# A soft mixture-of-experts kernel on Trainium2: the differences "kept P1 minus P5" on GpSimd instead of VectorE

## The chip, the cores and the metric

The kernel runs on one core of one Trainium2 chip. The metric is device time in microseconds (us) of one execution, as a median of runs. Engines are named as the profile names them: PE is TensorE's matmul, PEld its weight load, DVE is VectorE, ACT is ScalarE, POOL is GpSimd and SP is SyncE.

## The reference

Every token's output is the sum over all eight experts of the expert's matrix product, weighted by a softmax of the token's router logits:

```python
# x [16, 512, 512], router_logits [16, 512, 8], expert_weights [8, 512, 2048], all float32
probs = softmax(router_logits, axis=-1)
for e in range(8):
    output += probs[:, :, e:e+1] * np.matmul(x, expert_weights[e])
```

There are 8192 tokens (16 x 512), and the output is [16, 512, 2048] float32.

## The kernel before, in words

**The arithmetic.** Because the sum over experts can be put into the contraction, the output is one product of a matrix Z (the tokens times their probabilities, for all experts side by side) and a matrix W (the experts' weights on top of each other). The kernel computes it by a scheme of Strassen's kind, with seven products of blocks instead of eight, on two levels and in places on a third. The outer products are P1 to P7; `right[r]` is the weight operand of Pr, `lefts[r, q]` the token operand. q counts 16 groups of 512 tokens; each group has an even and an odd block of 256 tokens (`HQ`). Inside one outer product the same scheme is applied again: its seven inner steps are run in the order `STEPS = (1, 5, 6, 2, 7, 3, 4)`, and a step is eight matmuls of 128 x 128 by 128 x 512 in f16 into one PSUM bank (line 712).

**P1, P5 and P6.** Each outer product of one q has four result tiles of 128 x 512 f32, called tn = (0,0), (1,1), (0,1), (1,0). P1 is computed early and its results are written to DRAM (`kept`). Later come P5 and P6: P6's result is laid onto a base, which is kept P1 minus P5 for the same q, tile by tile. So for each q and each tn there is one subtraction of two 128 x 512 f32 tiles in SBUF, written in place over the tile with kept P1: 64 in all. `Base.fetch` (line 780) loads a tile of kept P1 with a DMA from SP's queue; `joined` (line 1171) makes the subtraction.

**Stages.** Work is a list of stages, and a stage is one or two outer products whose steps alternate. The stages of P5 and P6 (lines 1148 to 1152) are: P5 of q = 0 and 1; P6 of q = 0 alone; fourteen pairs of P6 of q and P5 of q + 1; P6 of q = 15 alone. In a pair the steps are numbered as slots 0 to 13, even slots for P6 and odd slots for P5; in a stage of one product slots are 0 to 6. `run` (line 1105) walks through the slots: hooks of that slot first, then the eight matmuls, then `slack` (which pops DVE tasks from the queue), then the step's `post`.

**Posts.** `post` takes a step's result out of PSUM. For a product without a base, such as P5, most are ACT copies to an SBUF tile (`post_alone`, line 723); for P6 (`post_on_base`, line 743) all but step 2 are DVE additions of a PSUM bank and the base. In one of the pair stages the DVE posts are those of slots 0, 2, 4, 8, 9, 10, 11 and 12. Step 1 of P6 needs base (0,0), step 5 needs (1,1), step 6 needs (0,1), step 4 needs (1,0). Steps 1, 6, 7 and 4 of one product share one PSUM bank: the matmuls of step 6 add onto what step 1 left there, those of step 7 onto step 6, and so on, with the post of each in between. So the post of slot 4 (step 6 of P6) has to have read the bank before the matmuls of slot 8 (step 7 of P6) write to it; in a stage of one product, the post of slot 2 before slot 4.

**What sets the order.** Every engine runs its instructions in program order. DVE's order is planned by hand: left operands, sums of weights and the like are tasks with a cost in us (`later`, line 388), held in a queue; `slack` (line 401) keeps a clock for PE and one for DVE and pops tasks as far as DVE's clock allows. `joined` puts its subtraction at the head of that queue (`True`) with a cost of 0.69; `need` (line 383) runs it at the latest when P6's post asks for the base. Hooks call `joined` in the stage before the P6 concerned at slot 12 for (0,0), at slot 13 for (1,1) and (0,1), and in P6's own stage at slot 3 for (1,0); where the stage before has one product, at slots 5, 6, 6 and again 3 (lines 1180 to 1182). The fetches of kept P1 are at slots 2, 4, 6 and 7 of the stage before (1, 2, 3, 4 in a stage of one product).

**POOL's queue** holds DMAs alone in these stages: the stores of result tiles to the output (`to_out`, line 771, one after each finished tile), the loads of x that still has to be cast (`XBlock.begin`, line 420), loads of weights for later sums (`load_part`, `cast_part`) and stores of weight sums. `pool` (line 126) and `note` (line 101) issue them in program order.

**Buffers.** Base tiles and result tiles come from one pool of 12 tiles (`hpool`, tag `h`); SP's fetch of a base waits until a tile of this pool is free, that is until a store has landed or a last reader is done. Matmul results have 6 + 2 PSUM banks (`bank`, tile name `ps`; `bank2`, `pt`).

Of the kernel before, what the change touches and what calls it, by code (L numbers as in the profile page):

```python
# [31 lines left out]
def kernel(  # L32
# [7 lines left out]
    nc = tc.nc  # L40
# [3 lines left out]
    ADD, SUB, MUL = mybir.AluOpType.add, mybir.AluOpType.subtract, mybir.AluOpType.mult  # L44
# [38 lines left out]
    def half():  # L83
        return h_tile([P, NB], f32)
# [16 lines left out]
    def note(i):  # L101
        last[i.ins.engine] = i.ins
        if ordered[0]:
            tc.keep_in_program_order(i)

    def dve(i):
        last[i.ins.engine] = i.ins
        tc.keep_in_program_order(i)
# [3 lines left out]
    def tt(o, a, b, op):  # L112
        dve(nc.vector.tensor_tensor(out=o, in0=a, in1=b, op=op))  # L113
# [12 lines left out]
    def pool(o, i, **how):  # L126
        note(nc.gpsimd.dma_start(out=o, in_=i, **how))  # L127
# [203 lines left out]
    for n in range(2):  # L331
# [23 lines left out]
        for j in range(4):  # L355
            o = half()
# [22 lines left out]
    def flush(task):  # L379
        while task is not None and not task.done:  # L380
            queue.popleft().run()

    def need(task):
        if task is not None and not task.done:
            flush(task)
            clock["pe"] = max(clock["pe"], clock["dve"])

    def later(cost, make, first=False):
        t = Task(cost, make)
        (queue.appendleft if first else queue.append)(t)  # L390
        return t
# [375 lines left out]
    def out_rows(q, odd, cols, tn):  # L767
        t, n = tn
        return out_f[ds((2 * q + odd) * HQ + t * HP, HP), ds(cols * NH + n * NB, NB)]

    def to_out(q, odd, cols, **how):
        return lambda tn, o: pool(out_rows(q, odd, cols, tn), o, **how)
# [28 lines left out]
    right = {r: Right() for r in (2, 5, 6, 7, 4, 3)}  # L801
    right[1] = Right(w, {p: Task(2.29, sums[p]) for p in (6, 7, 4)})
    lefts, xs, ps_, bases = {}, {}, {}, {}
# [6 lines left out]
    def left_of(r, q, fresh=True):  # L810
        a, b = 2 * q, 2 * q + 1
        if r == 1:
            pt = PBlock(a, P1, xp1[q - 2][1] if q in (2, 3) else None)
            if q in (2, 3):
                xs[a] = XBlock(a, xp1[q - 2][0])
            return Left(xblock(a), pt), [xblock(a), pt]
        if r == 2:
            pt = PBlock(a, P2)
            return Left(xblock(a), pt), [xblock(a), pt]
        if r == 7:  # L820
            pt = PBlock(b, P2)
            if q >= KEPT_Z:
                return Left(xblock(b), pt, kept=lefts[6, q]), [xblock(b), pt]
            return Left(xblock(b), pt, onto=ZHalves(q)), [xblock(b), pt]
        if r == 4:
            return Left(lefts[7, q].xb, lefts[7, q].pb), []
        if r == 5:
            pt = PBlock(b, PQ)
            return Left(xblock(b), pt), [xblock(b), pt]
        if r == 6:  # L830
            pt = PBlock(a, P1)
            return Left(xblock(a), pt, of=lefts[5, q]), [xblock(a), pt]
        if r == 3 and (q, 0) in EARLY:
            sources = {k: operand3[q, k] for k in range(2) if (q, k) in EARLY}
            if len(sources) == 2:
                return LoadedLeft(None, None, None, sources), []
            pa = PBlock(a, P2)
            return LoadedLeft(xblock(a), pa, ZHalf(q, z_places[q]), sources), [xblock(a), pa]
        if r == 3 and q < KEPT_Z:
            pt, kept_z = PBlock(a, P2), ZBlock(q)  # L840
            return Left(xblock(a), pt, kept=kept_z), [xblock(a), pt, kept_z]
        pa, pb = PBlock(a, PQ), PBlock(b, PQ)
        return Left(xblock(a), pa, (xblock(b), pb)), [xblock(a), pa, xblock(b), pb]

    def kept_rows(q):
        return lambda tn: kept[q][tn[1], ds(tn[0] * HP, HP), :]

    def product(r, q, **how):
        left, loads = left_of(r, q)
        lefts[r, q] = left  # L850
        p = None
        if r == 1:
            def sink(tn, o):
                pool(kept_rows(q)(tn), o)
            p = Product(right[1], left, sink)
        elif r == 2:
            if q >= ON_BASE or q in WITH_KEPT:
                bases[2, q] = Base(kept_rows(q))
            p = Product(right[2], left, to_out(q, 0, 0), bases.get((2, q)))
        elif r == 5:  # L860
            bases[6, q] = m1 = Base(kept_rows(q))
            m1.task = {}

            p = Product(right[5], left, to_out(q, 1, 0))
        elif r == 6:
            m1 = bases[6, q]

            def base(tn):
                need(m1.task[tn])
                return m1.t[tn]  # L870
            p = Product(right[6], left, to_out(q, 0, 1), base)
        elif r == 7:
            base = products[6, q].o.__getitem__
            if q < KEPT_Z:
                base = bases[7, q] = Base(lambda tn: out_rows(q, 0, 1, tn))
            p = Product(right[7], left, to_out(q, 1, 1), base)
        elif r == 4:
            p = Product(right[4], left, to_out(q, 1, 0, accum_op=ADD), products[7, q].o.__getitem__)
        else:
            p = Product(right[3], left, to_out(q, 0, 1, accum_op=ADD), **how)  # L880
        p.loads = loads
        products[r, q] = p
        return p

    products = {}
# [251 lines left out]
    for q in range(2, 16, 2):  # L1137
        add(product(1, q), product(1, q + 1))
    xs.clear()
    for q in (2, 4, 0, 6, 8, 10, 12, 14):  # L1140
        add(product(2, q), product(2, q + 1))
    for q in (*WITH_KEPT, *range(ON_BASE, 16)):
# [3 lines left out]
        fetch_at(k, 3, bases[2, q], INNER[3])  # L1146
    xs.clear()
    k5 = add(product(5, 0), product(5, 1))
    add(product(6, 0))
    for q in range(1, 15):  # L1150
# [18 lines left out]
    at(k6 - 1, 7, lambda: claim(products[5, 15].o, (1, 0)))  # L1169

    def joined(q, tn):
        m1 = bases[6, q]
        m1.task[tn] = later(0.69, lambda: tt(m1.t[tn], m1.t[tn], products[5, q].o[tn], SUB), True)

    for q in range(16):
        k = k5 + 1 + q
        duo = len(stages[k - 1]) == 2
        for slot, tn in zip((2, 4, 6, 7) if duo else (1, 2, 3, 4), INNER):
            fetch_at(k - 1, slot, bases[6, q], tn)
        for tn, where in zip(INNER, ((k - 1, 12), (k - 1, 13), (k - 1, 13), (k, 3)) if duo  # L1180
                             else ((k - 1, 5), (k - 1, 6), (k - 1, 6), (k, 3))):
            at(*where, lambda q=q, tn=tn: joined(q, tn))
# [264 lines left out]
    for stage, slot, q, k in ((k3 - 1, 2, 11, 0), (k3 - 1, 5, 11, 1), (k3 - 1, 7, 8, 0), (k3 - 1, 9, 5, 0),  # L1447
                              (k3 - 1, 10, 8, 1), (k3 - 1, 12, 5, 1)):
        left = lefts[3, q]
# [191 lines left out]
```

## Time and profile before

| what | value |
|---|---|
| median of 3 runs | 1351.62 us (1351.12 to 1351.67) |
| the profiled execution's own time | 1351.78 us |
| its span, first to last instruction | 1350.1 us |
| PE, DVE, ACT, POOL busy in the span | 1344.0, 1166.9, 281.9, 403.9 us |
| granted TensorE clock | 1.0 |
| moved by DMA | 346.26 MB |

The profile is of one execution and its times are read against 1351.78 us, not against the median: 1.7 us of that lie before and after the span. A line of a group gives the kernel's line, the engine, the operation, the tiles written and read (buffer numbers left out), the shapes and the count; then the busy time in us and the mean duration of one in ns; then the engine's idle time just before these instructions and what ended it. L113 is the helper through which all DVE additions and subtractions go, L127 the helper of POOL's DMAs, L136 the helper of the matmuls, so groups are told apart by their tiles. A line of a timeline gives the start and the duration in us, then the instruction; instructions of one kind that follow each other are merged and counted.

### The profile page before, as it was taken

How to read it: one execution, taken by the hardware profiler on the slowest of the kernel's cores; microseconds unless marked ns; L12 is line 12 of the kernel's file. 1: busy time of each engine (PE TensorE's matmuls, PEld its weight loads, DVE VectorE, ACT ScalarE, POOL GpSimd, SP SyncE). 2: the span in 40 equal slices, each digit the busy share in tenths (PEclk: the TensorE clock that was granted, in tenths of full speed). 3: DMA queues.
4: the chain of work that ended last, by engine and by line, in shares of the span. 5: the costliest groups of instructions: out<-in, count | busy, mean ns of one | idle time of the engine just before them, and what ended most of it. 6: DMA issues, size and time to landing. Idle time of an engine off the chain costs nothing.

```text
span 1350.1 us, 19508 instructions
## 1 busy us (share of the span) xinstructions
PE 1344.0 (100%) x7122; PEld 694.3 (51%) x7122; DVE 1166.9 (86%) x1483; ACT 281.9 (21%) x593; POOL 403.9 (30%) x619
## 2 busy tenths in 40 slices
PE   9999999999999999999999999999999999999998
PEld 4465655565544444444444444554555455556564
DVE  7878898989989889797897889889898989898984
ACT  3342423223211111111111100110111111224331
POOL 3123322333323232323312112424334231232342
PEclk9999999999999999999999999999999999999999
DMA  9999989989899999999998889999999989999997
GB/s 181 242 222 240 239 264 242 291 284 290 247 329 282 323 288 286 295 306 265 318 325 265 295 313 189 243 239 216 244 249 226 219 219 310 308 178 230 262 163 132
DMA packets 185392, 346.26 MB, mean 256 GB/s; under 512 B 52176, under 2 KB 81616, under 8 KB 181200
## 3 DMA queue, kind: packets, MB, share of 16 engines
q0 software_dynamic: 84960, 176.72, 58.0%
q1 hardware_dynamic: 97024, 146.15, 35.4%
q10 hardware_dynamic: 3312, 22.15, 4.6%
q8 instruction: 55, 0.90, 0.3%
q14 instruction: 41, 0.34, 0.1%
HBM read 203.19 MB, written 174.26 MB: 280 GB/s over the span
## 4 chain that ended last, share of the span: by engine, by line
PE 98%; DMA 1%; POOL 0%; issue 0%; ACT 0%; POOLq 0%
PE ps L136 77%; PE pt L136 21%; DMA w<-in_expert_weights_dram 1%; POOL w L127 0%; ACT h L1578 0%; POOL ident L234 0%; POOLq L234 0%; POOLq L1625 0%
## 5 line engine op out<-in xcount | busy, mean ns | idle before, releaser
L136 PE MATMUL ps<-w,z 128*128 128x512 f16 (+1 forms) x3884 | 840.0, 372 | 0.0
L136 PEld LDWEIGHTS <-z 128*128 128x128 f16 x5236 | 512.3, 98 | 538.1 <-issue 1.1
L127 POOL DMA_DIRECT2D out_dram<-h x380 | 251.8, 679 | 723.9 <-ACT h L751 321.9
L113 DVE TENSOR_TENSOR h<-ps,h 128x512 f32<-128x512 f32 x318 | 214.9, 686 | 59.1 <-PE ps L136 58.0
L136 PE MATMUL pt<-w,z 128*128 128x512 f16 (+1 forms) x1304 | 253.2, 338 | 0.7 <-DMA w<-in_expert_weights_dram 0.7
L113 DVE TENSOR_TENSOR z<-xT,pT 128x2048 f16<-128x2048 f16 x188 | 226.8, 1217 | 2.2 <-DMA xT<-xs 2.2
L136 PE MATMUL ps<-w,d 128*128 128x512 f16 x880 | 200.7, 379 | 0.0
L738 ACT COPY h<-ps 128x512 f32<-128x512 f32 x102 | 59.8, 586 | 394.0 <-PE ps L136 394.0
L136 PEld LDWEIGHTS <-d 128*128 128x128 f16 x880 | 86.1, 98 | 96.3
L113 DVE TENSOR_TENSOR z<-z,d 128x2048 f16<-128x2048 f16 x110 | 131.8, 1217 | 0.0
L113 DVE TENSOR_TENSOR w<-w 128x1024 f16<-128x1024 f16 (+2 forms) x106 | 116.1, 1114 | 2.6 <-PE ps L136 1.0
L113 DVE TENSOR_TENSOR d<-z 128x1024 f16<-128x1024 f16 x110 | 74.1, 685 | 1.0
L113 DVE TENSOR_TENSOR h<-pt,h 128x512 f32<-128x512 f32 x75 | 51.3, 687 | 27.0 <-PE pt L136 23.9
L751 ACT COPY h<-ps 128x512 f32<-128x512 f32 x54 | 31.6, 586 | 203.5 <-PE ps L136 203.5
L113 DVE TENSOR_TENSOR ps<-ps,h 128x256 f32<-128x256 f32 (+1 forms) x84 | 50.6, 603 | 21.0 <-PE ps L136 15.1
L734 ACT COPY h<-ps 128x512 f32<-128x512 f32 x89 | 49.9, 599 | 70.1 <-PE ps L136 61.3
L127 POOL DMA_DIRECT2D kept<-h x56 | 30.6, 547 | 86.2 <-DVE h L113 48.7
L113 DVE TENSOR_TENSOR z<-z 128x2048 f16<-128x2048 f16 (+1 forms) x52 | 50.5, 978 | 1.5
L730 ACT COPY ps<-ps 128x512 f32<-128x512 f32 x47 | 26.8, 570 | 107.4 <-PE ps L136 59.5
L113 DVE TENSOR_TENSOR h<-h 128x512 f32<-128x512 f32 (+2 forms) x69 | 45.0, 675 | 0.1
L127 POOL DMA_DIRECT2D out_dram<-kept x40 | 42.0, 1150 | 0.2 <-issue 0.2
L136 PEld LDWEIGHTS <-h 128*128 128x128 f16 x384 | 37.6, 98 | 4.3
(109 smaller groups left out, 691.7 us busy)
## 6 DMA issues: line engine op xcount, KB each, us to landing
out_dram<-h POOLq DMA_DIRECT2D x380, 256.0 KB, 7.5
z<-z SPq DMA_DIRECT2D x56, 512.0 KB, 8.7
pT<-p_dram SPq DMA_DIRECT2D x93, 256.0 KB, 8.1
h<-kept SPq DMA_DIRECT2D x88, 256.0 KB, 7.2
w<-wd ACTq DMA_DIRECT2D x20, 1024.0 KB, 8.6
w<-in_expert_weights_dram POOLq DMA_DIRECT2D x33, 512.0 KB, 12.2
xT<-x SPq DMA_DIRECT2D x63, 256.0 KB, 7.8
h<-out_dram SPq DMA_DIRECT2D x60, 256.0 KB, 8.9
```

The costliest lines, as they stand in the source:

```text
L113: dve(nc.vector.tensor_tensor(out=o, in0=a, in1=b, op=op))
L127: note(nc.gpsimd.dma_start(out=o, in_=i, **how))
L136: note(nc.tensor.matmul(ps, z, w, start=start, stop=stop, skip_group_check=True))
L730: act(nc.scalar.copy(self.banks["b"], x))
L734: act(nc.scalar.copy(o[tn], q if p == 5 else x))
L738: act(nc.scalar.copy(o[TN[p]], b if p == 2 else x))
L751: act(nc.scalar.copy(o[tn], b))
```

## The change

The 64 subtractions are issued on GpSimd, directly at their hooks, and no longer pass through the queue of DVE tasks. With that, the tasks kept per tile of the base (`m1.task`) and the function that asked for them before a post go away; a post of P6 gets the tile and waits, on the engine, for the instruction that wrote it.

```diff
         elif r == 5:
-            bases[6, q] = m1 = Base(kept_rows(q))
-            m1.task = {}
-
+            bases[6, q] = Base(kept_rows(q))
             p = Product(right[5], left, to_out(q, 1, 0))
         elif r == 6:
-            m1 = bases[6, q]
-
-            def base(tn):
-                need(m1.task[tn])
-                return m1.t[tn]
-            p = Product(right[6], left, to_out(q, 0, 1), base)
+            p = Product(right[6], left, to_out(q, 0, 1), bases[6, q])
...
     def joined(q, tn):
-        m1 = bases[6, q]
-        m1.task[tn] = later(0.69, lambda: tt(m1.t[tn], m1.t[tn], products[5, q].o[tn], SUB), True)
+        o = bases[6, q].t[tn]
+        note(nc.gpsimd.tensor_tensor(out=o, in0=o, in1=products[5, q].o[tn], op=SUB))
```

The hooks and their slots, the fetches of kept P1 and everything else stay as they are. In POOL's program order a subtraction now stands where its hook stands: that of (0,0) behind the store that follows the post of slot 11, those of (1,1) and (0,1) between the stores that follow the posts of slots 12 and 13, that of (1,0) behind the loads that the early slots of P6's stage issue.

## The prediction

> **What bounds the kernel now.** First the page: engine shares, the chain that ended last, and the row of base loads, needed below.
>
> ```profile
> span 1350.1 us, 19508 instructions
> ## 1 busy us (share of the span) xinstructions
> PE 1344.0 (100%) x7122; PEld 694.3 (51%) x7122; DVE 1166.9 (86%) x1483; ACT 281.9 (21%) x593; POOL 403.9 (30%) x619
> ...
> PE 98%; DMA 1%; POOL 0%; issue 0%; ACT 0%; POOLq 0%
> ...
> h<-kept SPq DMA_DIRECT2D x88, 256.0 KB, 7.2
> ```
>
> PE is busy all the time and is the chain. A busy matmul row can still hide a slow pipeline, so I next read the stretch in which the change acts: the fourteen pair stages of P6 and P5, from 428.7 to 767.1 us, in the view of windows, and then the same stretch grouped by form.
>
> ```profile
> 428.70:767.10 338.40, 338.40 (x1569) 153.43 (x1568) 287.86 (x350) 48.42 (x83) 95.45 (x168) 1.00 0.99 296
> ```
> ```profile
> L136 PE MATMUL ps<-w,z 128*128 128x512 f16 x897 | 198.3, 379 | 0.0
> ...
> L136 PE MATMUL pt<-w,z 128*128 128x512 f16 x448 | 101.3, 379 | 0.0
> ...
> L136 PE MATMUL ps<-w,d 128*128 128x512 f16 x224 | 50.6, 379 | 0.0
> ```
>
> The columns of the window are its length, then PE, PEld, DVE, ACT and POOL busy, the granted clock, DMA share and GB/s. The three groups are all of the window's 1569 matmuls, with 0.0 us idle before each: 338.40 / 1569 = 215.7 ns from one to the next. So a slot of eight takes 1.725 us, a pair stage of 14 slots 24.2 us, and no wait of PE is left in the stretch. DVE is busy for 287.86 of 338.40 us, 85%, yet nothing waits for it long enough to stop PE. **Taking work from DVE can therefore give PE nothing back here**; the question is whether the new place makes PE wait.
>
> **Where a pair stage has slack.** I take the stage that begins at 622 us; DVE first, from its timeline.
>
> ```profile
> 619.28 0.68 DVE L113 TENSOR_TENSOR h<-h 128x512 f32<-128x512 f32 x1
> 620.35 0.69 DVE L113 TENSOR_TENSOR h<-ps,h 128x512 f32<-128x512 f32 x1 [0.38 <-PE ps L136]
> 620.95 1.28 DVE L113 TENSOR_TENSOR h<-h 128x512 f32<-128x512 f32 x2
> 622.15 1.22 DVE L113 TENSOR_TENSOR z<-z,d 128x2048 f16<-128x2048 f16 x1
> 623.80 0.70 DVE L113 TENSOR_TENSOR ps<-ps,h 128x512 f32<-128x512 f32 x1 [0.43 <-PE ps L136]
> 624.41 1.22 DVE L113 TENSOR_TENSOR z<-z,d 128x2048 f16<-128x2048 f16 x1
> 625.54 1.22 DVE L113 TENSOR_TENSOR z<-xT,pT 128x2048 f16<-128x2048 f16 x1
> 626.79 1.23 DVE L113 TENSOR_TENSOR z<-z 128x2048 f16<-128x2048 f16 x1
> 627.93 0.68 DVE L113 TENSOR_TENSOR h<-pt,h 128x512 f32<-128x512 f32 x1
> 628.53 0.68 DVE L113 TENSOR_TENSOR h<-h 128x512 f32<-128x512 f32 x1
> 629.13 0.69 DVE L113 TENSOR_TENSOR d<-z 128x1024 f16<-128x1024 f16 x1
> 629.74 1.22 DVE L113 TENSOR_TENSOR z<-xT,pT 128x2048 f16<-128x2048 f16 x1
> 630.99 1.22 DVE L113 TENSOR_TENSOR z<-z 128x2048 f16<-128x2048 f16 x1
> 632.13 0.68 DVE L113 TENSOR_TENSOR h<-ps,h 128x512 f32<-128x512 f32 x1
> ```
> ```profile
> 632.23 6.64 PE L136 MATMUL ps<-w,z 128*128 128x512 f16 x30
> ```
>
> The four `h<-h` are one q's subtractions, in the order (0,0), then (1,1) and (0,1), then (1,0). The posts of slots 0, 2 and 4 are at 623.80, 627.93 and 632.13. The PE row begins with slot 6, so slot 8 begins at 632.23 + 2 x 1.725 = 635.68. There step 7 of P6 writes to the bank that the post of slot 4 reads until 632.13 + 0.68 = 632.81. That post may thus come **2.87 us later** before PE stops; it is the tightest of the early posts, since post 0 guards slot 4 and post 2 slot 10.
>
> **The change part by part.** Removed from DVE: 64 instructions of about 0.68 us, 44 us in all. They stood beside PE's work, so on the path to the end this is worth 0. What moves up behind them is `z<-z,d` and the operands of the next stage, for which nobody waits.
>
> Added to POOL: 64 subtractions. No trace row shows GpSimd doing one. The nearest rows are its only arithmetic and a fill of one element:
>
> ```profile
> 2.67 0.33 POOL L234 TENSOR_SCALAR_AFFINE_SELECT ident<-ident 128x128 f16<-128x128 f16 x1
> 0.38 0.10 POOL L1625 MEMSET const-bfloat16-1.0<- 128x1 bf16 x1
> ```
>
> (0.33 - 0.10) / 128 = 1.8 ns for an element of one input. For 512 elements that is 0.10 + 0.93 = 1.03 us; if two inputs are read in turn, 0.10 + 2 x 0.93 = 1.97 us. The lower end is DVE's 0.68. I take d = 1.03 us, the nearest row's, and keep 0.68 and 1.97 for the range. [...]
>
> POOL's queue around the same stage:
>
> ```profile
> 619.66 0.54 POOL L127 DMA_DIRECT2D out_dram<-h  x1 [1.24 <-DVE h L113]
> 621.33 0.54 POOL L127 DMA_DIRECT2D out_dram<-h  x1 [1.13 <-DVE h L113]
> 622.95 0.54 POOL L127 DMA_DIRECT2D out_dram<-h  x1 [1.08 <-ACT h L738]
> ...
> 627.06 0.71 POOL L127 DMA_DIRECT2D w<-in_expert_weights_dram  x1 [0.32 <-DMA out_dram<-h]
> ```
>
> Subtraction (0,0) queues behind the first store, (1,1) and (0,1) stand between the second and the third, and (1,0) behind the loads that end at 627.77. The trace of before has no GpSimd arithmetic beside DVE's, so it cannot tell whether the two hinder each other. I cost it the hard way: a subtraction and a DVE operation with both inputs in SBUF never overlap, the later one waits for the other's end, and posts (one input in PSUM) run freely. With d = 1.03:
>
> - (0,0) from 620.20 to 621.23, beside the post at 620.35. The first `z<-z,d` may start at 621.23, earlier than before, and ends at 622.45.
> - (1,1) from 622.45 to 623.48, (0,1) from 623.48 to 624.51. The post of slot 0 at 623.80 has its base.
> - The second `z<-z,d` starts at 624.51 instead of 624.41, so all behind it is 0.10 us late; the post of slot 2 at 628.03 finds (1,1) done long ago.
> - The third store issues at 624.51 instead of 622.95, and what follows it ends at about 629.31. There (1,0) starts, ends at 630.34, and holds back the `z<-xT,pT` that before began at 629.74: 0.6 us late, in which the 0.68 us of the removed subtraction is already used up.
> - The post of slot 4 ends 0.6 us later. Allowed are 2.87. **PE loses 0.**
>
> So the pair stages cost nothing. The two stages with P6 alone are tighter; of the first:
>
> ```profile
> 416.38 1.07 POOL L127 DMA_DIRECT2D out_dram<-h  x2 [2.45 <-DVE h L113]
> ```
> ```profile
> 421.80 0.68 DVE L113 TENSOR_TENSOR h<-ps,h 128x512 f32<-128x512 f32 x1
> ```
> ```profile
> 421.58 2.75 PE L136 MATMUL ps<-w,z 128*128 128x512 f16 x12
> ```
>
> PE's row begins with slot 3, so slot 4 begins at 423.31, and the post of slot 2 (421.80 to 422.48) has 0.83 us left. (0,0) runs from 416.92 to 417.95, after the first of the stores; then a store, and (1,1) from 418.49 to 419.52. It holds back the `z<-z,d` behind the post of slot 0 by some 0.6 us, (0,1) holds back the next `z<-xT,pT` again, in all 1.1 us: the post ends at 423.58 and PE waits 0.3 us. The other such stage, at 767 us, I take as equal, an estimate. Sum: 0 + 2 x 0.3 = **0.6 us**. Against the profiled execution that is 1351.8 + 0.6 = 1352.4 us; its 1351.78 lies 0.16 us above the median of 1351.62, so the forecast for a median is **1352.2 us**, which is no change. A measurement of this kernel can tell about 0.2%, 2.7 us, from no change. The forecast's own range is 1351.1 to 1354.3, the upper end for d = 1.4.
>
> **The rivals.**
>
> *The shared work costs more (slower).* The same schedule with d = 1.97: (0,0) ends at 622.17, (1,1) runs from 623.39 to 625.36, (0,1) from 626.58 to 628.55, and each pushes a `z` operation before it can go on itself. `z<-xT,pT` starts at 628.55 instead of 625.54, (1,0) takes 633.37 to 635.34, and the post of slot 4 is 4.35 us late: it ends at 637.16, and PE stops for 1.48 us. Times 14 that is 20.7 us; the single stages lose about 3.1 us each: 27 us, 1378. Between d = 1.03 (0.6 late) and 1.97 (4.35 late) the 2.87 us are used up at d = 1.6, and from there the fourteen stages pay; the single stages alone reach 2.7 us at d = 1.4. For it: DVE runs operations with two SBUF inputs back to back from slot 0 to slot 7, just where three of the four subtractions fall. Against it: posts and idle gaps separate them, and if the engines do not hinder each other at all, DVE only gains time. [...] Chance 0.34.
>
> *POOL's queue backs up (slower).* Stores come late, tiles of the pool free late, and SP fetches bases late:
>
> ```profile
> 603.59 1.78 SPq L124 DMA_DIRECT2D h<-kept  x2
> ```
>
> These two are the last of the q whose subtractions begin at 619.28. Issued by 605.37 and with 7.2 us to land, both are there at about 612.6. A store shifts by 1.6 us (622.95 to 624.51); if the fetches shift as much, 5 us of margin remain even for the first subtraction. POOL would be busy for 95.45 + 56 x 1.03 = 153 of 338.40 us, 45%; at d = 1.97, 61%. It would need delays of over 5 us in POOL's order; each microsecond beyond that delays a post in 14 stages, and 1 us beyond what the 2.87 us cover gives 1366. Chance 0.05.
>
> *DVE's relief shows (faster).* PE would need waits to lose. It has 0.0 us of them in the stretch, and in the whole span 1350.1 - 1344.0 = 6.1 us at most; half of that would give 1348.6. I see no mechanism by which the change would reach them. Chance 0.02.
>
> **How the numbers follow.** Forecast 0.59, the costlier sharing 0.34, POOL's queue 0.05, faster 0.02. Slower by over 0.2%: 0.34 + 0.05 = 0.39; within 0.2%: 0.59; faster: 0.02. Range: 1351.0 to 1366 us. The lower end is a change that costs nothing, read as low as the lowest run of before (1351.12), and leaves out the faster case; the upper end is the sharing rival at d = 1.8 (an excess of 0.2 x 4 = 0.8 us in each of 14 stages, 11, and some 2 x 2.5 for the single ones). Beyond it lies perhaps a third of that rival and half of the queue's.
>
> **What would show it.** Right, if: PE's groups keep 0.0 us idle between 428.7 and 767.1 us, and that stretch stays at 338.4; the POOL subtractions take 1.0 to 1.4 us; DVE's busy time falls by 44 us; the post of slot 4 ends less than 2.87 us after its old place. Wrong, if: PE rows show idle time released by DVE at slots 8 of pair stages (sharing), `z` operations on DVE become longer than 1.22 us or have idle time before them ended by POOL (the two do block each other, at a larger price), POOL's subtractions take over 1.6 us, or DVE posts wait for POOL (queue).

## The result, and the profile after

The changed kernel takes **1367.57 us** (median of four runs, 1366.17 to 1370.21); the kernel before 1351.61 (1351.12 to 1351.67). The ratio is 1.0121, with a 95% interval of 1.0103 to 1.0139: slower by 1.2%, 16 us. The prediction on record was 1352.2 us, no change, with 1351.0 to 1366 as its range. The profiled execution of the changed kernel took 1368.85 us.

The page of the changed kernel, first: span, engine shares, the chain that ended last, two groups of matmuls with idle time, and the groups of subtractions and of one kind of operand.

```profile
span 1367.1 us, 19543 instructions
...
PE 1345.8 (98%) x7122; PEld 694.1 (51%) x7122; DVE 1187.8 (87%) x1419; ACT 282.0 (21%) x593; POOL 499.2 (37%) x683
...
PE 93%; DMA 3%; DVE 2%; issue 1%; POOL 1%; ACT 0%; DVEq 0%; POOLq 0%; SPq 0%
...
L136 PE MATMUL ps<-w,z 128*128 128x512 f16 (+1 forms) x3884 | 840.8, 372 | 6.8 <-DVE h L113 6.8
...
L136 PE MATMUL ps<-w,d 128*128 128x512 f16 x880 | 202.3, 381 | 7.1 <-DVE ps L113 7.1
L113 DVE TENSOR_TENSOR z<-z,d 128x2048 f16<-128x2048 f16 x110 | 160.9, 1488 | 0.0
...
L1166 POOL TENSOR_TENSOR h<-h 128x512 f32<-128x512 f32 x64 | 95.9, 1511 | 0.7
```

Two things stand out. PE now waits, and both waits end with DVE, not with POOL. And DVE has 64 instructions fewer (1419 for 1483) and is busy for **longer**: 1187.8 us for 1166.9. The `z<-z,d` operations take 1488 ns on average. Here are the groups of DVE in the changed kernel, with their shapes kept apart:

```profile
L113 DVE TENSOR_TENSOR h<-ps,h 128x512 f32<-128x512 f32 x318 | 214.4, 685 | 61.7 <-PE ps L136 58.6 <-issue 1.9 <-DMA out_dram<-h 1.0
...
L113 DVE TENSOR_TENSOR z<-z 128x2048 f16<-128x2048 f16 x36 | 54.1, 1502 | 1.2
```

and the same groups of the kernel before:

```profile
L113 DVE TENSOR_TENSOR h<-ps,h 128x512 f32<-128x512 f32 x318 | 214.9, 686 | 59.1 <-PE ps L136 58.0 <-issue 0.9
L113 DVE TENSOR_TENSOR z<-z,d 128x2048 f16<-128x2048 f16 x110 | 131.8, 1217 | 0.0
...
L113 DVE TENSOR_TENSOR z<-z 128x2048 f16<-128x2048 f16 x36 | 44.1, 1225 | 1.2
```

Operations with both inputs in SBUF became longer (`z<-z,d` by 29.1 us in all, `z<-z` by 10.0); the posts, `h<-ps,h`, which read one input from PSUM, did not: 685 and 686 ns. The stretch of the pair stages, in the view of windows of the changed kernel (columns as in the prediction):

```profile
428.70:767.10 338.40, 331.30 (x1532) 149.61 (x1530) 297.62 (x286) 47.85 (x82) 176.51 (x220) 1.00 0.95 287
```

It holds 1532 matmuls where the kernel before had 1569. 37 x 0.2157 = 8.0 us of PE's time are gone there, at a full clock of 1.00. To see all of the loss, I set the start of each matmul beside that of the same matmul before, and take the growth of the delay: 2.37 us in the stage of P6 q = 0 alone, 8.22 in the pair stages (seven stops of 0.49 to 2.05 us, in five of the fourteen stages), 6.37 in the stage of P6 q = 15 alone. That is 16.96 of the 17.0 us between the spans (1367.1 - 1350.1); the rest is in the first 20 us, where the two traces differ by some tenths (the first `pt<-w,z` starts at 9.97 us before and at 10.57 in the changed kernel).

**One stop from the inside.** The largest is in the stage of q = 15. The timeline of the changed kernel, DVE, then POOL, then PE:

```profile
776.90 6.07 DVE L113 TENSOR_TENSOR w<-w 128x2048 f16<-128x2048 f16 x1
782.89 2.28 DVE L113 TENSOR_TENSOR z<-z,d 128x2048 f16<-128x2048 f16 x1
785.10 0.69 DVE L113 TENSOR_TENSOR ps<-ps,h 128x512 f32<-128x512 f32 x1
...
776.68 0.54 POOL L127 DMA_DIRECT2D out_dram<-h  x1 [1.19 <-DVE h L113]
777.23 1.28 POOL L1166 TENSOR_TENSOR h<-h 128x512 f32<-128x512 f32 x1
778.44 0.56 POOL L127 DMA_DIRECT2D out_dram<-h  x1
779.03 2.50 POOL L1166 TENSOR_TENSOR h<-h 128x512 f32<-128x512 f32 x2
...
785.83 3.49 PE L136 MATMUL ps<-w,d 128*128 128x512 f16 x8 [4.61 <-DVE ps L113]
```

Read it from the end. PE waits 4.61 us (4.77 by the starts of its matmuls, whose rows are 0.16 us longer than the place that each takes) at slot 2 of this stage of one product, for the post of slot 0, `ps<-ps,h`, which ran from 785.10. The post's own base, subtraction (0,0), had been ready at 778.51. What it stood behind is DVE's order: first `w<-w`, which takes 1.22 us when nothing is in its way and here took **6.07**, through three subtractions and a store; then `z<-z,d`, 2.28 us. So the post was not held itself; it was queued behind operations that were. In the kernel before, the same post stood ahead of both:

```profile
768.84 0.70 DVE L113 TENSOR_TENSOR ps<-ps,h 128x512 f32<-128x512 f32 x1 [0.76 <-PE ps L136]
769.45 1.22 DVE L113 TENSOR_TENSOR w<-w 128x2048 f16<-128x2048 f16 x1
...
771.18 1.22 DVE L113 TENSOR_TENSOR z<-z,d 128x2048 f16<-128x2048 f16 x1
```

**Why DVE's order changed.** The diff took 64 tasks of 0.69 us out of the queue. The planner's clock for DVE is then up to four times 0.69 us earlier, so `slack` lets more tasks go before the next post. The pair stage of which the prediction gave the timeline shows the same, in the changed kernel: both `z<-z,d` now stand ahead of the post of slot 0, where before one did. The second of them, held for 2.29 us, ends just before the post.

```profile
626.07 6.26 DVE L113 TENSOR_TENSOR z<-z,d 128x2048 f16<-128x2048 f16 x1
...
634.47 0.69 DVE L113 TENSOR_TENSOR ps<-ps,h 128x512 f32<-128x512 f32 x1
...
625.95 0.54 POOL L127 DMA_DIRECT2D out_dram<-h  x1 [0.63 <-DMA wd<-w]
626.51 1.28 POOL L1166 TENSOR_TENSOR h<-h 128x512 f32<-128x512 f32 x1
...
628.30 2.50 POOL L1166 TENSOR_TENSOR h<-h 128x512 f32<-128x512 f32 x2
...
635.21 3.61 PE L136 MATMUL ps<-w,d 128*128 128x512 f16 x16 [1.22 <-DVE ps L113]
...
642.92 0.59 PE L136 MATMUL ps<-w,z 128*128 128x512 f16 x2 [0.65 <-DVE h L113]
```

The last row is slot 8: PE stops a second time, for the post of slot 4. The new order adds to its delay too, since a `z<-xT,pT` (641.05) now stands ahead of that post which before stood behind it. Of the seven stops in the pair stages two are of the first kind, at slot 4 (2.81 us by the starts), four of the second, at slot 8 (4.94), and one is at slot 12 (0.49).

### The profile page after: what moved, and what is told of

It reads as the page before. It is cut to its first block, busy times and chain, and to the rows that moved or that the text cites. A ratio compares the mean times of both kernels' runs of the same rounds, so it can differ in the third digit from the quotient of the medians.

```text
span 1367.1 us, 19543 instructions
## 1 busy us (share of the span) xinstructions
PE 1345.8 (98%) x7122; PEld 694.1 (51%) x7122; DVE 1187.8 (87%) x1419; ACT 282.0 (21%) x593; POOL 499.2 (37%) x683
## 4 chain that ended last, share of the span: by engine, by line
PE 93%; DMA 3%; DVE 2%; issue 1%; POOL 1%; ACT 0%; DVEq 0%; POOLq 0%; SPq 0%
PE ps L136 73%; PE pt L136 20%; DMA out_dram<-h 1%; DMA h<-kept 1%; DVE z L113 1%; DVE h L113 1%; DMA w<-in_expert_weights_dram 1%; POOL h L1166 0%; DVE w L113 0%; POOL out_dram L127 0%; POOL wd L127 0%; DVE d L113 0%; POOL w L127 0%; DVE ps L113 0%; DVE u L113 0%
## 5 line engine op out<-in xcount | busy, mean ns | idle before, releaser
L113 DVE TENSOR_TENSOR z<-xT,pT 128x2048 f16<-128x2048 f16 x188 | 236.4, 1268 | 2.1 <-DMA xT<-xs 2.1
L113 DVE TENSOR_TENSOR z<-z,d 128x2048 f16<-128x2048 f16 x110 | 160.9, 1488 | 0.0
L113 DVE TENSOR_TENSOR w<-w 128x1024 f16<-128x1024 f16 (+2 forms) x106 | 126.0, 1210 | 5.6 <-DMA wd<-w 3.0
L1166 POOL TENSOR_TENSOR h<-h 128x512 f32<-128x512 f32 x64 | 95.9, 1511 | 0.7
L113 DVE TENSOR_TENSOR z<-z 128x2048 f16<-128x2048 f16 (+1 forms) x52 | 60.5, 1170 | 1.6
L127 POOL DMA_DIRECT2D wd<-w x45 | 24.5, 546 | 49.0 <-DVE w L113 47.8
```

Source lines behind the costliest of these rows:

```text
L1166: note(nc.gpsimd.tensor_tensor(out=o, in0=o, in1=products[5, q].o[tn], op=SUB))
```

## The experiments

Three things had changed at once: who reads SBUF (GpSimd beside DVE), the order of DVE's work, and the load of POOL's queue. My theory after reading the trace was that the reads hold DVE's operations and that the new order puts a post behind them. The rivals were that the new order alone does it, that POOL's queue does it, and that GpSimd's writes or its time do it. The first four kernels take these apart.

**No subtraction at all, the order of after.** P6's base is kept P1 alone.

```diff
     def joined(q, tn):
-        o = bases[6, q].t[tn]
-        note(nc.gpsimd.tensor_tensor(out=o, in0=o, in1=products[5, q].o[tn], op=SUB))
+        pass
```

> This kernel leaves the 64 subtractions out: P6 is laid onto kept P1 alone. DVE's order is that of the changed kernel. Sharing (GpSimd's reads hold DVE's operations with two SBUF inputs): no hold is left, 1351.0 to 1352.5 us. Order (the planner, without 64 costs of 0.69 us, now puts z<-z,d and w<-w ahead of the post of slot 0, and that alone stops PE): as slow as the changed kernel, 1364 to 1369. Queue (POOL's stores and loads come late behind the subtractions): 1351.0 to 1352.5, as the first.

Measured: 1351.87 us (1351.45 to 1352.67), ratio 1.000 (0.999 to 1.0009). DVE's timeline has the order of after, both `z<-z,d` ahead of the post, and the window of the pair stages is full:

```profile
621.54 2.35 DVE L113 TENSOR_TENSOR z<-z,d 128x2048 f16<-128x2048 f16 x2
624.39 0.70 DVE L113 TENSOR_TENSOR ps<-ps,h 128x512 f32<-128x512 f32 x1 [0.50 <-PE ps L136]
```
```profile
428.70:767.10 338.40, 338.40 (x1570) 153.38 (x1569) 255.74 (x295) 48.37 (x83) 95.19 (x168) 1.00 0.99 296
```

What follows: the new order does no harm by itself, since two unheld `z<-z,d` take 2.35 us and the post then waits for PE. It also shows the other side: DVE has 32 us less to do in this stretch (255.74 for 287.86) and the time is the same. Freeing DVE is worth nothing here.

**The subtraction on GpSimd, but planned as before**, as a task of 0.69 us in DVE's queue. Against the kernel before, whose `m1.task` and `need` are kept:

```diff
-        m1.task[tn] = later(0.69, lambda: tt(m1.t[tn], m1.t[tn], products[5, q].o[tn], SUB), True)
+        m1.task[tn] = later(0.69, lambda: note(nc.gpsimd.tensor_tensor(out=m1.t[tn], in0=m1.t[tn],
+                            in1=products[5, q].o[tn], op=SUB)), True)
```

> The subtractions are on GpSimd, but issued through the queue of DVE tasks at their old cost of 0.69 us, so DVE's other operations stand in the order of the kernel before. Sharing alone: DVE is held as often as in the changed kernel, 1362 to 1368 us. Order alone: 1351.5 to 1353. Both together (a hold costs PE only where an operation that is held stands ahead of a post): in between, 1353 to 1360, with the stall of 4.8 us at 781 us gone.

Measured: 1361.99 us (1360.32 to 1363.63), ratio 1.0076 (1.0059 to 1.0093). The pair stages lose 0.0 us, but the two single stages 4.37 and 4.49. In the trace DVE's other operations stand in the order of the kernel before, one by one. The timeline of the second, POOL, DVE, PE:

```profile
772.60 4.92 POOL L1173 TENSOR_TENSOR h<-h 128x512 f32<-128x512 f32 x4
...
776.34 0.70 DVE L113 TENSOR_TENSOR ps<-ps,h 128x512 f32<-128x512 f32 x1 [6.14 <-POOL h L1173]
...
777.10 2.37 PE L136 MATMUL ps<-w,d 128*128 128x512 f16 x8 [2.64 <-DVE ps L113]
```

The total comes to the edge of what sharing alone was expected to give, but this is another loss than that of after. Each task goes to the head of the queue, so those put in last come out first: (0,0), which the first post needs, is the third of the four, which run behind a store issued at 772.05, and starts only when two others of 1.23 us are done. The post waits for POOL itself (6.14 us idle, ended by POOL). On DVE the same order was harmless: three in 1.89 us from 766.19, ahead of the post. So this kernel answers for the pair stages alone: with the order of before, and the subtractions where DVE's queue would have them, they lose nothing, although operations are still held. In the stage of the prediction's timeline, the one that stopped PE twice in after, it is nearly as long a hold as there:

```profile
624.95 5.74 DVE L113 TENSOR_TENSOR z<-z,d 128x2048 f16<-128x2048 f16 x1
```

The post of slot 0 follows it at 630.61, with the second `z<-z,d` behind the post, and PE does not stop.

**Writes alone.** In place of the subtraction GpSimd fills the tile in two halves; it reads nothing, and P6's base is zeros.

```diff
-        note(nc.gpsimd.tensor_tensor(out=o, in0=o, in1=products[5, q].o[tn], op=SUB))
+        for c in (ds(0, NB // 2), ds(NB // 2, NB // 2)):
+            note(nc.gpsimd.memset(o[:, c], 0.0))
```

> In place of each subtraction GpSimd fills the base tile with zeros in two halves, so P6 has no base; GpSimd writes and reads nothing. DVE's order is that of the changed kernel. Sharing by reads: DVE's operations keep 1.22 us, 1351.0 to 1353 us. Sharing by writes too: z<-z,d stays at 1.4 us or more in the mean, 1356 to 1367. Queue: POOL is nearly as busy as in the changed kernel, 1356 to 1367 with DVE's operations at 1.22 us.

Measured: 1352.18 us (1351.58 to 1355.79), ratio 1.0004 (0.9995 to 1.0014). The groups:

```profile
L1167 POOL MEMSET h<- 128x256 f32 x128 | 36.1, 334 | 0.0
...
L113 DVE TENSOR_TENSOR z<-z,d 128x2048 f16<-128x2048 f16 x110 | 130.9, 1215 | 0.0
```

No operation of DVE is longer than before, and PE loses nothing. POOL has 128 more instructions in the same places, and posts that wait for them. So neither writes nor additional entries in POOL's queue are the cause; **GpSimd's reads** are what is left. The two halves take 0.67 us, though, half of a subtraction, so POOL's time was not matched here; a later kernel settles that.

**The two engines alone** (a kernel of its own: rows of GpSimd subtractions of 128x512 f32 beside DVE operations, and nothing else of the computation).

```python
for i in range(6): sub(i)        # GpSimd, b <- b - a
for i in range(16): wide()       # DVE, 128x2048 f16, both inputs in SBUF
```

> No part of the reference's work: only short series on DVE and GpSimd. GpSimd subtractions of 128x512 f32 alone: 1.28 us each. Beside DVE operations of 128x2048 f16 with two SBUF inputs: if the second to come waits for the first, DVE and GpSimd take turns and 6 subtractions lengthen a series of 16 operations by up to 6 x 1.28 = 7.7 us; if GpSimd keeps the path while its queue is full, one DVE operation is held through all of them, 7 us or more in one piece, and the rest run at 1.2. Beside DVE operations with one input in PSUM and beside fills: no DVE operation longer than alone. With a store between the subtractions: a DVE operation gets in at each store if the path is let go there.

The kernel took 134.72 us. The groups where GpSimd has no one beside it give 1.26 us a subtraction; side by side with `wide`, and then with an operation that reads PSUM and SBUF (`k<-ps,a`):

```profile
35.01 8.84 POOL L82 TENSOR_TENSOR b<-b,a 128x512 f32<-128x512 f32 x4
...
33.77 8.95 DVE L75 TENSOR_TENSOR o<-z,z 128x2048 f16<-128x2048 f16 x5
```
```profile
59.20 7.40 POOL L82 TENSOR_TENSOR b<-b,a 128x512 f32<-128x512 f32 x6
...
58.88 9.65 DVE L79 TENSOR_TENSOR k<-ps,a 128x512 f32<-128x512 f32 x16
```

Four subtractions in 8.84 us (2.20 each) against six in 7.40 (1.23 each): with two SBUF inputs on both sides the engines take strict turns, a subtraction and an operation, each shown as 2.24 and 2.28 us long because the wait is within. With a PSUM input there is no effect: sixteen at 0.60 us each. That is the sharing which the prediction assumed, and its size d is 1.26 us. But turns give 2.28 us at most, not the 6.07 and 6.26 of the changed kernel. So something of the long holds is still missing.

**The prediction's own schedule.** Subtractions at the hooks on GpSimd, and for each an empty task of 0.69 us, so that DVE keeps the order of before (in the trace it does, operation by operation). Against the kernel before:

```diff
-        m1.task[tn] = later(0.69, lambda: tt(m1.t[tn], m1.t[tn], products[5, q].o[tn], SUB), True)
+        note(nc.gpsimd.tensor_tensor(out=m1.t[tn], in0=m1.t[tn], in1=products[5, q].o[tn], op=SUB))
+        m1.task[tn] = later(0.69, lambda: None, True)
```

> The subtractions are issued on GpSimd at their hooks as in the changed kernel, and a task that does nothing is put into the queue of DVE tasks at 0.69 us for each, so DVE's other operations stand in the order of the kernel before. This is the schedule that the prediction worked out by hand, at d = 1.28 us. Order theory: the fourteen pair stages lose 0 and the two stages with P6 alone 1 to 3 us together, 1352.5 to 1355 us. Sharing alone: the holds cost the same in any order, 1364 to 1369.

Measured: 1358.41 us (1356.13 to 1359.53), ratio 1.0048 (1.0033 to 1.0063), more than the 1352.5 to 1355 expected. The kernel before, in 13 runs beside it, had a median of 1351.91 and two runs of 1354.07 and 1356.20. In the profiled execution (1356.13) PE loses 2.32 us in the first single stage, 1.23 in the pair stages and 1.32 in the last. A pair stage of its timeline, DVE and POOL:

```profile
697.49 6.16 DVE L113 TENSOR_TENSOR z<-z,d 128x2048 f16<-128x2048 f16 x1
703.58 0.69 DVE L113 TENSOR_TENSOR ps<-ps,h 128x512 f32<-128x512 f32 x1
...
696.67 1.14 POOL L127 DMA_DIRECT2D out_dram<-h  x2 [1.19 <-DVE h L113]
697.83 1.28 POOL L1173 TENSOR_TENSOR h<-h 128x512 f32<-128x512 f32 x1
...
699.62 2.49 POOL L1173 TENSOR_TENSOR h<-h 128x512 f32<-128x512 f32 x2
```

What follows: with the order of before, the loss in this execution, the lowest of four, is 4.9 us in place of 17.0 (6.5 by the medians, in place of 16.0). The long holds are there all the same: in three pair stages a `z<-z,d` is held through three subtractions (4.97 to 6.16 us), where the trace of after has two such stages. The first single stage loses as much as in after. So the order is the larger factor in the pair stages (8.22 to 1.23) and in the last stage (6.37 to 1.32), and none in the first.

**The pair stages alone.** The order of after for q = 1 to 14; q = 0 and 15 as before, on DVE. Against the kernel before, whose line `m1.task[tn] = later(...)` this replaces:

```diff
+        if q in (0, 15):
+            m1.task[tn] = later(0.69, lambda: tt(m1.t[tn], m1.t[tn], products[5, q].o[tn], SUB), True)
+        else:
+            note(nc.gpsimd.tensor_tensor(out=m1.t[tn], in0=m1.t[tn], in1=products[5, q].o[tn], op=SUB))
+            m1.task[tn] = None
```

> As the changed kernel for q = 1 to 14; the subtractions of q = 0 and 15, which belong to the two stages with P6 alone, stay on DVE as before. If the stalls add up as the trace of the changed kernel has them (8 us in pair stages, 9 us with the slow matmuls in the two single ones): 1358 to 1361 us. If a late DVE is carried from stage to stage, so that the single stage's loss comes from the pair before it: 1351.5 to 1356.

Measured: 1359.59 us (1356.91 to 1362.58), ratio 1.0059 (1.0043 to 1.0075); PE loses 8.93 us in the pair stages and nothing in the single ones. That is near after's 8.22, so the losses of the stages add up.

**The same load of POOL at another time.** As the last, with the hooks of q = 2 to 14 moved to slots 9, 11 and 12 of the stage before and slot 9 of P6's own.

```diff
-        for tn, where in zip(INNER, ((k - 1, 12), (k - 1, 13), (k - 1, 13), (k, 3)) if duo
+        for tn, where in zip(INNER, ((k - 1, 9), (k - 1, 11), (k - 1, 12), (k, 9)) if 1 < q < 15
+                             else ((k - 1, 12), (k - 1, 13), (k - 1, 13), (k, 3)) if duo
```

> As the run with q = 0 and 15 on DVE, and the subtractions of q = 2 to 14 hooked at slots 9, 11, 12 and, in P6's own stage, 9, where DVE does posts and idles. Sharing with order: hardly any operation is held, 1351.0 to 1353 us. If POOL's queue were the cause (stores late), nothing gained against that run: 1357 to 1361.

Measured: 1351.64 us (1350.86 to 1352.8), ratio 0.9996 (0.9986 to 1.0005). The window of the pair stages, and the group of `z<-z,d`:

```profile
428.70:767.10 338.40, 338.40 (x1570) 153.40 (x1569) 278.51 (x296) 48.33 (x83) 167.35 (x223) 1.00 0.99 297
```
```profile
L113 DVE TENSOR_TENSOR z<-z,d 128x2048 f16<-128x2048 f16 x110 | 148.3, 1374 | 0.0
```

POOL is busy for 167.35 us, close to the 176.51 of after, with as many subtractions in these stages, and PE loses nothing. DVE's order is that of the kernel just above, operation by operation. So POOL's time and the length of its queue are not the cause either: it is **which DVE operations** the subtractions fall beside. `z<-z,d` is still 157 ns longer on average than before, and four operations are held for 3.4 to 3.9 us, but PE stops for none of them. And the kernel is no faster than before: the place found is free, not a gain.

**Loads and stores among the subtractions** (a kernel of its own).

> No part of the reference's work. Short series: GpSimd does a subtraction, a store, two subtractions and a store, with or without three casting loads of x in front; DVE does 1 to 6 operations with one input in PSUM and then three with two SBUF inputs, either plain 128x2048 f16 or with the strides and the broadcast of z<-z,d. Taking turns: no DVE operation is longer than 2.5 us anywhere. Queue depth (GpSimd's instructions that wait ready in line keep the path): DVE operations of 4 us and more where loads stand in front. Strides: 4 us and more only with the strided form.

It took 363.5 us and decided nothing. Its stores read the tile that DVE's short operations write, so DVE waited for landings (165.2 us idle, ended by `out_dram<-k`), and the two engines hardly met.

**Planned order and DVE for the single stages**, the two remedies of the fifth and sixth kernels together.

```diff
+        if q in (0, 15):
+            m1.task[tn] = later(0.69, lambda: tt(m1.t[tn], m1.t[tn], products[5, q].o[tn], SUB), True)
+        else:
+            note(nc.gpsimd.tensor_tensor(out=m1.t[tn], in0=m1.t[tn], in1=products[5, q].o[tn], op=SUB))
+            m1.task[tn] = later(0.69, lambda: None, True)
```

> Both cures together: the charge that keeps DVE's order, and the subtractions of q = 0 and 15 on DVE; 56 subtractions stay on GpSimd at their hooks. From the trace of the charged kernel, the pair stages lost 1.2 us there and the two single ones 3.6. If these losses are local: 1352 to 1354 us. If the charge only moved a loss: 1356 to 1360.

Measured: 1354.45 us over six runs, from 1351.93 to 1357.41; ratio 1.0027 (1.0015 to 1.0039), just over the 1352 to 1354 expected. The profiled one, 1352.01, loses 1.02 us in the pair stages. This is the prediction's schedule in the fourteen stages where it forecast a loss of 0, and against the 1351.38 of the kernel before it costs 0.6 to 6.0 us, another amount in each run, 3.1 by the median. The same 56 subtractions in the order of after cost 7.7 by the median (1359.59 against 1351.91): that is the fairer measure of what the order is worth in the pair stages, since the traced run of this kernel is one of its two fastest.

**When does DVE get in?** (a kernel of its own: rows of four subtractions, the DVE operation asking at -0.05 to +1.28 us of the first, with and without a store behind the first, plain or with the strides of `z<-z,d`).

> No part of the reference's work. In each of 48 short series GpSimd does four subtractions in a row, with or without a store behind the first, and DVE a PSUM copy of growing length and then two operations with two SBUF inputs, so the first of these asks at a different point of the first or second subtraction. Taking turns at every end of a subtraction: the longest DVE operation is 1.2 + 1.3 us in every series, whatever the point. As in the full kernel (an operation that asks early is held through all of the row, one that asks late gets in at the next end): 4 to 6.5 us for some points, 2.5 us at most for others, and the store makes room for the late ones only.

The kernel took 387.35 us. In all 48 rows DVE gets in at the next end of a subtraction; the longest operation took 2.29 us. Strides make no difference (1920 ns on average with them, 1919 without), nor does a store between subtractions: those rows stay within the 2.29 us too. My reason for the long holds at that time, subtractions that follow each other closely, was wrong.

**A store just ahead** (the last, with 0, 1 or 2 stores issued on GpSimd right before a row of three subtractions, DVE asking from -2.33 to +1.31 us of the first).

```python
for i in range(lead): put(i)     # GpSimd, store, lead = 0, 1, 2
sub(0)
if mid: put(2)
sub(1); sub(2)
```

> No part of the reference's work. Series as in the run with 48 of them, where every DVE operation got in at the next end of a subtraction; but 0, 1 or 2 stores are issued on GpSimd just ahead of the first of three subtractions, with or without a store between the first and the second. [...]

The kernel took 498.19 us. Two rows of it that differ in the store ahead, with DVE asking 0.11 and 0.07 us after the first subtraction's start. The first row's first subtraction and DVE operation, then the second's store, three subtractions and DVE operation:

```profile
34.70 1.26 POOL L82 TENSOR_TENSOR b<-b,a 128x512 f32<-128x512 f32 x1
...
34.81 2.23 DVE L75 TENSOR_TENSOR o<-z,z 128x2048 f16<-128x2048 f16 x1
...
205.02 0.56 POOL L114 DMA_DIRECT2D out_dram<-st  x1
205.60 3.70 POOL L82 TENSOR_TENSOR b<-b,a 128x512 f32<-128x512 f32 x3
...
205.67 4.72 DVE L75 TENSOR_TENSOR o<-z,z 128x2048 f16<-128x2048 f16 x1
```

Without a store ahead none of 22 rows had an operation over 2.29 us. With one, 27 of 44 had one of 4.12 to 5.82 us: it is held through **all three** subtractions, each of which takes its unheld 1.27 us, and ends 1.09 us after the last one's end; a store between the subtractions does not let it in either, as with the `w<-w` of 6.07 us in the changed kernel, which ran on through the store at 778.44. In 26 of them DVE's first operation asked from 0.46 us before the first subtraction to 0.67 after it, and no operation that was first to ask in this span got a turn. Where the first one asked earlier than that, the two engines took turns, with one exception; no row with a store ahead had it ask later. In the changed kernel subtraction (0,0) stands behind a store, and the two operations held longest asked 0.44 and 0.33 us before it. The traces of the six full kernels with subtractions on GpSimd hold 31 rows of two or more subtractions directly behind a store, where DVE's first operation with two SBUF inputs asked within the same span: 25 of them were held, for 2.91 to 6.26 us, and six got in after one subtraction at most (1.40 to 2.64 us).

## Why the prediction was wrong

Loss of PE against the kernel before in the profiled executions, from the starts of its matmuls, in us:

| kernel | first single stage | pair stages | last single stage |
|---|---|---|---|
| after | 2.37 | 8.22 | 6.37 |
| order of before, through DVE's queue (its loss is a wait for POOL) | 4.37 | 0.0 | 4.49 |
| order of before, at the hooks | 2.32 | 1.23 | 1.32 |
| q = 1 to 14 alone | 0.0 | 8.93 | 0.0 |
| order of before at the hooks, q = 1 to 14 alone | 0.0 | 1.02 | 0.0 |
| q = 1 to 14, other slots | 0.0 | 0.0 | 0.0 |
| fills, or no subtraction | 0.0 | 0.0 | 0.0 |

Each row is one traced execution, set against one trace of the kernel before; the kernels ran on three chips, each beside runs of the kernel before.

- **"Taking work from DVE can therefore give PE nothing back here"**: right. The kernel without subtractions is at a ratio of 1.000.
- **d = 1.03 us**: too small, but within the bounds. An unheld subtraction took 1.26 to 1.28. By the prediction's own two points (0.6 us late at 1.03, 4.35 at 1.97) that makes the post of slot 4 some 1.6 us late, less than the 2.87 allowed: 0 in the pair stages and about 1 us in each single one, 2 in all. The size of d is not what failed.
- **"A subtraction and a DVE operation with both inputs in SBUF never overlap, the later one waits for the other's end, and posts run freely"**: half right, and the first step that failed. Posts do run freely (686 ns before, 685 after), fills do not hinder (`z<-z,d` at 1215 ns beside them), and the engines do take turns where no store stands ahead (2.29 us at most in the short series). But behind a store DVE mostly does not get its turn (25 of 31 rows in the full kernels): it waits for two or three subtractions and the store among them, up to 6.26 us for 1.22. With the prediction's own order this costs 6.5 us by the medians (the fifth kernel), where turns at the measured d would cost 2. The working had let each `z` operation in between two subtractions. The condition, two SBUF inputs on DVE beside a subtraction on GpSimd, is what the runs show (`z<-z,d` 1488 ns for 1217); that the later one waits for the other's end holds for the turns of 2.28 us and not for the holds of 4 to 6.
- **"What moves up behind them is `z<-z,d` and the operands of the next stage, for which nobody waits"**: the second step that failed, and the larger one. I read the timeline of before and took the 64 instructions out, as if the order of the others stayed. The code makes the order from the costs of the queue's tasks, and with 64 costs gone it placed more held operations ahead of the posts of slots 0 and 4. Nobody waits for `z<-z,d`; the post that stands behind it does have someone waiting. Keeping the old order takes the whole loss from 16.0 to 6.5 us by the medians, and that of the pair stages from 8.22 to 1.23 in the traces, from 7.7 to 3.1 by the medians.
- **"The tightest of the early posts" is that of slot 4**: the place was largely right. Four of the seven stops in the pair stages, 4.94 of 8.22 us, are at slot 8 for that post, which the prediction had named as a sign of being wrong; it came later than its slack allowed (2.87 us in the stage shown). In the order of after the post of slot 0 became tight as well: in the stage shown, PE stopped 1.22 us for it at 635.21, and 4.61 us in the last stage.
- **The single stages, "2 x 0.3 us"**: measured 2.37 and 6.37. In the first stage the place was right, slot 4, and the price is that of a hold through two subtractions, in either order (a `z<-xT,pT` of 4.35 us in after, a `z<-z,d` of 3.76 in the order of before). "The other such stage, at 767 us, I take as equal" failed: PE stopped there two slots earlier. In the order of before its first post ended at 769.54, 0.82 us ahead of slot 2 (770.36), and in after two held operations stood ahead of that post. 1.6 of its 6.37 us are slow matmuls after the stop (below).
- **The rivals**: the sharing rival named the mechanism, the engine and the sign, and put its price at 27 us from d = 1.97 and its start at d = 1.6. At the measured d it gives 2 us; the price came from holds and order, not from d. The upper end of the range, drawn from this rival, was also added wrongly: its 11 us and 2 x 2.5 us on top of 1351.6 are 1367.6, not 1366. So it is no credit to the sums that the measured 1367.57 comes out so near. POOL's queue was rightly put low: in the changed kernel no wait of DVE or POOL ends with a load of kept P1, and as many subtractions on POOL cost nothing at other slots.

Not shown is why a store ahead makes the difference: the runs give only when a hold comes and how long it is. Nor did the last kernel reproduce all cases of the big one: an operation that asked 0.28 us into a subtraction behind two stores got its turn there (2.09 us at 479.52), and no row tried just that; in the kernel with q = 1 to 14 alone the same operation, asking at the same point, was held for 5.10 us (476.34). So the span is where a hold is likely, not a rule without exceptions. If the holds differ between runs of one kernel, that may be why the kernel with both remedies scatters from 1351.93 to 1357.41; I have one trace of it, so this is argued only.

## What to carry to other kernels

Elementwise work moved from VectorE to GpSimd cost nothing here beside VectorE work that reads PSUM (686 ns before, 685 after), and beside work with two SBUF inputs only where the held operations had time left (ratio 0.9996 at the other slots, against 1.0059). Before such a move, look for each operation with two SBUF inputs that runs in the same stretch (here `z<-z,d`, from 1217 to 1488 ns on average), and for who is queued behind it, not only for who reads its result. Where an order is computed from costs, taking a cost out moves everything else: compare the new order before pricing the old one. And where the bounding engine has no idle time, relief for another engine is worth 0 from the start (here 32 us less of VectorE's work in the pair stages, at a ratio of 1.000), so the change can only be judged by what it may break.

## What the hardware showed that I had not expected

- **The long hold**: in the series alone, a VectorE operation of 1.22 us that was first to ask, from 0.46 us before to 0.67 us after the start of the first GpSimd subtraction behind a store, took 4.1 to 5.8 us (three subtractions); in the full kernels 25 of 31 such were held, for up to 6.26 us. The subtractions themselves lose nothing then (1.27 us each).
- **A stop of PE can cost more than its length.** The windows of the changed kernel right after its stops of 2.37 and 4.77 us show it by the granted clock, the last but two of the columns:

```profile
425.80:427.50 1.70, 1.70 (x8) 0.76 (x8) 1.07 (x1) 0.00 (x0) 0.00 (x0) 1.00 0.95 243
785.80:789.30 3.50, 3.47 (x9) 1.23 (x9) 2.93 (x3) 0.00 (x0) 0.00 (x0) 0.53 0.00 0
```

By their rows, the eight matmuls after the first stop took 1.89 us and those after the second 3.49: 427 ns in place of 216 from one to the next, 1.6 us more. The two stops of the kernel with the subtractions in DVE's queue (2.68 and 2.80 us) were followed by such matmuls too, after six at full speed, which made 2.68 into 4.37 and 2.80 into 4.49; the granted clock was 0.80 in the window 422.00:424.30 of that kernel and 0.69 in 777.10:780.50. The longest stop without slow matmuls behind it was 2.37 us, the shortest with them 2.68.
